# Rotary embedding on one core: a pair of slabs loaded in two halves of 64 partitions, the next pair in one load, and one table form for all slabs

## The chip, the core and the metric

The kernel runs on one NeuronCore of a Trainium2 chip. Its engines are TensorE (PE), VectorE (DVE), ScalarE (ACT), GpSimd (POOL) and SyncE (SP), each with an instruction stream of its own. 16 DMA engines move data between the memory outside the core (HBM) and the core's SBUF, which has 128 partitions. A DMA is cut into descriptors, each of which moves one contiguous run of bytes; the trace records each as a packet. DMAs are issued from an engine's stream: here the loads of x from SP, and the tables' loads and all stores from ACT. The metric is device time in microseconds (us), lower is better; a comparison is made on the median of several runs.

## The reference

A rotary position embedding: x is a float32 array of 16 batches x 512 positions x 1024 columns, seen as 16 heads of 64 columns. Each head's first 32 columns (x1) and last 32 (x2) are turned by a table of cosines and sines with one row for each position (512 x 32 each). x and the output are 33.55 MB each.

```python
x = x.reshape(batch, seq, num_heads, head_dim)
x1, x2 = x[..., :half_dim], x[..., half_dim:]
cos = cos[None, :, None, :]
sin = sin[None, :, None, :]
rotated = np.concatenate([
    x1 * cos - x2 * sin,
    x1 * sin + x2 * cos
], axis=-1)
```

## The kernel before

The 16 batches are worked on as 8 slabs of two batches, 4.19 MB each. On the 128 partitions a slab is a tile of 128 x 8192 float32 (`W`), 32 KB for each partition, that is 8 rows of x (`rpp`).

There are two layouts. Slabs 0, 1, 6 and 7 are contiguous in HBM: partition p holds rows 8p to 8p+7 of the slab (`dram`). Slabs 2 and 3, and 4 and 5, are halves of a pair: a pair is 8.39 MB, partition p holds 16 rows of it, 64 KB, and the two slabs are the first and the second 32 KB of each partition (`paired`). Two slab buffers (`slabs`, 32 KB a partition each) and two pair buffers (`pairs`, 64 KB each) take 192 KB of each partition.

Loads, all issued from SP: slabs 0 and 1 (line 68), then slabs 2 and 3 by one DMA whose descriptors are 64 KB (line 87), then 4 and 5 by one DMA each in 32 KB descriptors (line 90). These need no wait. Slabs 6 and 7 use the buffers of 0 and 1 again, so SP holds each of their loads until the store of slab 0, or 1, has landed (line 68 again, called from line 188).

Tables: cos and sin are loaded from ACT's queue into 64 partitions (line 83), 1 KB for each. POOL builds selection matrices (`pick`, `pick2`, lines 93 to 112) and casts the tables to bf16 (line 116). PE multiplies them so that each partition gets the rows that its positions need, with the sine's sign turned for the first half. There are two such tables: `tab` for the contiguous slabs (line 121, copied out by DVE at line 127), and `tab2` for both halves of a pair (line 133, copied out by ACT at line 172).

Passes: slab 0, 6 and 7 are worked on in two passes of 4 rows, the others in one pass of 8. A pass is a cast of the slab from float32 to bf16 in place on ACT (line 157), two multiplications by the tables and one addition on DVE (lines 175 and 176), and a cast back to float32 on ACT (line 179). ACT's order is fixed: the cast of the next pass comes before the cast back of this one. So when the next slab has not landed, the cast back of the present slab and its store wait behind it. After the last pass of a slab ACT issues its store (lines 182 to 186): 0, 1, 2, 3, 6 and 7 alone in 32 KB descriptors, 4 and 5 together in 64 KB descriptors.

Of the kernel before, what the change touches and what calls it, by code (L numbers as in the profile page):

```python
# [9 lines left out]
@with_exitstack  # L10
def kernel(
    ctx: ExitStack,
    tc: tile.TileContext,
    x: bass.AP,
    cos: bass.AP,
    sin: bass.AP,
    num_heads: int,
    out: bass.AP,
):
    nc = tc.nc  # L20
    P = nc.NUM_PARTITIONS

    batch, seq, dim = x.shape
    nh = num_heads
    hd = dim // nh
    half = hd // 2
    bf16 = mybir.dt.bfloat16
    f32 = mybir.dt.float32

    nb = 2  # L30
    nslabs = batch // nb
    rpp = nb * seq // P
    W = rpp * dim
    SP = seq // rpp
    TW = rpp * half

    out_flat = out.rearrange("b s h d -> b s (h d)")

    singles = ctx.enter_context(tc.tile_pool(name="singles", bufs=1))
    slabs = ctx.enter_context(tc.tile_pool(name="slabs", bufs=2))  # L40
    pairs = ctx.enter_context(tc.tile_pool(name="pairs", bufs=2))
    psum = ctx.enter_context(tc.tile_pool(
        name="psum", bufs=1, space=bass.MemoryType.PSUM))


    def dram(t, s, a=0, n=W):
        return bass.AP(tensor=t.tensor, offset=t.offset + s * nb * seq * dim + a,
                       ap=[[W, P], [1, n]])


    def view(t, offset, *dims):
        return dataclasses.replace(t, offset=t.offset + offset,
                                   ap=[t.ap[0], *[list(d) for d in dims]])

    slab = {}


    def paired(t, s, a=0, n=2 * W):
        return bass.AP(tensor=t.tensor, offset=t.offset + s * nb * seq * dim + a,
                       ap=[[2 * W, P], [1, n]])


    def load(s):
        slab[s] = slabs.tile([P, W], f32, tag="slab", name="slab")
        nc.sync.dma_start(out=slab[s], in_=dram(x, s))  # L68


    def place(s):
        t = pairs.tile([P, 2 * W], f32, tag="pair", name="pair")
        slab[s], slab[s + 1] = view(t, 0, (1, W)), view(t, W, (1, W))
        return t


    load(0)


    cos_sb = singles.tile([SP, TW], f32, tag="cos_sb")  # L80
    sin_sb = singles.tile([SP, TW], f32, tag="sin_sb")
    for t, src in ((cos_sb, cos), (sin_sb, sin)):
        nc.scalar.dma_start(out=t, in_=bass.AP(
            tensor=src.tensor, offset=src.offset, ap=[[TW, SP], [1, TW]]))

    load(1)
    nc.sync.dma_start(out=place(2), in_=paired(x, 2))
    pair = place(4)
    for h in range(2):
        nc.sync.dma_start(out=slab[4 + h], in_=paired(x, 4, h * W, W))  # L90


    pick = singles.tile([SP, 2 * P], bf16, tag="pick")
    nc.gpsimd.memset(pick, 0.0)  # L94
    for g in range(2):
        part = view(pick, g * P, (SP, P // SP), (1, SP))
        nc.gpsimd.affine_select(  # L97
            out=part, in_=part, compare_op=mybir.AluOpType.not_equal,
            fill=1.0 - 2.0 * g, base=0, pattern=[[0, P // SP], [-1, SP]],
            channel_multiplier=1)  # L100

    pick2 = singles.tile([SP, 4 * P], bf16, tag="pick2")
    nc.gpsimd.memset(pick2, 0.0)  # L105
    for h in range(2):
        for g in range(2):
            part = view(pick2, (2 * h + g) * P, (SP // 2, 2 * P // SP), (1, SP // 2))
            nc.gpsimd.affine_select(  # L109
                out=part, in_=part, compare_op=mybir.AluOpType.not_equal,  # L110
                fill=1.0 - 2.0 * g, base=-h, pattern=[[0, 2 * P // SP], [-2, SP // 2]],
                channel_multiplier=1)

    tab1 = singles.tile([SP, 2 * TW], bf16, tag="tab1")
    for i, t in enumerate((cos_sb, sin_sb)):
        nc.gpsimd.tensor_copy(out=view(tab1, i * TW, (1, TW)), in_=t)  # L116

    acc = psum.tile([P, 2 * rpp * hd], f32, tag="acc")
    for i in range(2):
        for h in range(2):  # L120
            nc.tensor.matmul(  # L121
                view(acc, i * rpp * hd + h * half, (hd, rpp), (1, half)),
                view(pick, i * h * P, (1, P)),
                view(tab1, i * TW, (half, rpp), (1, half)),
                start=True, stop=True)
    tab = singles.tile([P, 2 * rpp * hd], bf16, tag="tab")
    nc.vector.tensor_copy(out=tab, in_=acc)  # L127

    acc2 = psum.tile([P, 4 * rpp * hd], f32, tag="acc2")
    for i in range(2):  # L130
        for r in range(2):
            for h in range(2):
                nc.tensor.matmul(  # L133
                    view(acc2, (2 * i + r) * rpp * hd + h * half, (hd, rpp), (1, half)),
                    view(pick2, (2 * r + i * h) * P, (1, P)),
                    view(tab1, i * TW, (half, rpp), (1, half)),
                    start=True, stop=True)
    tab2 = singles.tile([P, 4 * rpp * hd], bf16, tag="tab2")

    passes = []
    for s in range(nslabs):
        n = rpp if 1 <= s < nslabs - 2 else rpp // 2
        passes += [(s, r, n) for r in range(0, rpp, n)]


    def halves(u):
        s, r, n = u  # L150
        t = view(slab[s], 0, (1, W)).bitcast(bf16)
        return [view(t, (2 * r + i * n) * dim, (1, n * dim)) for i in range(2)]


    def cast(u):
        s, r, n = u
        nc.scalar.copy(out=halves(u)[0], in_=view(slab[s], r * dim, (1, n * dim)))  # L157


    def factor(u, i):  # L160
        s, r, n = u
        t, a = (tab2, (2 * i + s % 2) * rpp * hd) if 2 <= s < 6 else (tab, i * rpp * hd)
        return view(t, a + r * hd, (hd, n), (0, nh), (1, hd))


    cast(passes[0])
    for i, u in enumerate(passes):
        s, r, n = u
        if i + 1 < len(passes):
            cast(passes[i + 1])  # L170
        if i == 0:
            tc.keep_in_program_order(nc.scalar.copy(out=tab2, in_=acc2))  # L172
        lo, up = halves(u)
        for k, t in enumerate((up, lo)):
            nc.vector.tensor_mul(out=t, in0=lo, in1=factor(u, k))  # L175
        nc.vector.tensor_add(  # L176
            out=up, in0=up, in1=view(lo, half, (hd, n * nh), (-half, 2), (1, half)))

        nc.scalar.copy(out=view(slab[s], r * dim, (1, n * dim)), in_=up)  # L179
        if r + n == rpp:  # L180
            if s == 5:
                nc.scalar.dma_start(out=paired(out_flat, 4), in_=pair)
            elif s in (2, 3):
                nc.scalar.dma_start(out=paired(out_flat, 2, (s - 2) * W, W), in_=slab[s])
            elif s != 4:
                nc.scalar.dma_start(out=dram(out_flat, s), in_=slab[s])
            if s < 2:
                load(s + 6)

# [34 lines left out]
```

## Time and profile before

| what | value |
|---|---|
| median of 3 runs | 166.65 us (164.38 to 167.47) |
| the profiled execution, whole | 161.82 us |
| its span from first to last instruction | 160.0 us |
| ACT busy | 115.1 us |
| DVE busy | 108.4 us |
| PE busy | 2.9 us |
| packets on the load queue | 1008, 33.55 MB |
| packets on ACT's queue (stores and tables) | 1168, 33.69 MB |

The profile is of one execution. Lines of the page name the source line (L157), the engine, the operation, what it writes and reads, its busy time, and the idle time of its engine before it with what ended it. Engine names with a q (SPq, ACTq) stand for the engine's instruction queue, which issues DMAs. "us to landing" is the time from a DMA's issue until its completion was signalled; it includes waiting behind other DMAs of its queue. Rows by stretch give, after the bounds and the length, the busy time of PE, PE's weight loads, DVE, ACT and POOL with their instruction counts, then the granted TensorE clock, the mean busy share of the 16 DMA engines and the GB/s that they moved. A packet is counted in the stretch in which it starts, so short stretches can show more than 1.0.

### The profile page before, as it was taken

The page shows a single profiled execution, that of the slowest core. Times are in us where ns is not written, and L with a number is a line of the kernel's source. Part 1 is how long each engine was busy: PE and PEld are TensorE (multiplying, and loading weights), DVE is VectorE, ACT ScalarE, POOL GpSimd, SP SyncE. Part 2 cuts the span into 40 slices and gives each one's busy share as a digit, 9 for nine tenths or more (in the row PEclk, how much of TensorE's full clock was granted, in tenths as well). Part 3 has the DMA queues.
Part 4 walks back from the last instruction along what each step waited for, and adds up shares of the span by engine and source line. Part 5 has one row for each costly group of instructions (what it writes and reads, how often), then busy time and mean ns, then how long its engine had stood idle before and what let it go on. Part 6 is the DMA issues. An engine that isn't in the chain of part 4 may idle for free.

```text
span 160.0 us, 179 instructions
## 1 busy us (share of the span) xinstructions
PE 2.9 (2%) x12; PEld 1.6 (1%) x12; DVE 108.4 (68%) x34; ACT 115.1 (72%) x24; POOL 3.3 (2%) x14
## 2 busy tenths in 40 slices
PE   0001410000000000000000000000000000000000
PEld 0000300000000000000000000000000000000000
DVE  0000299999971999899899989999279399910000
ACT  3005979994099999999999999399993999380000
POOL 6000000000000000000000000000000000000000
DMA  7999999699699999999999999999998998999994
GB/s 246 410 410 410 393 524 491 295 524 491 295 393 491 426 393 442 459 410 418 459 434 393 475 442 393 450 459 401 442 491 377 524 410 377 393 459 459 393 450 205
DMA packets 2176, 67.24 MB, mean 420 GB/s; under 512 B 256, under 2 KB 384, under 8 KB 384
## 3 DMA queue, kind: packets, MB, share of 16 engines
q1 hardware_dynamic: 1008, 33.55, 49.3%
q10 hardware_dynamic: 1168, 33.69, 48.8%
HBM read 33.69 MB, written 33.55 MB: 420 GB/s over the span
## 4 chain that ended last, share of the span: by engine, by line
DMA 67%; ACT 13%; issue 5%; DVE 4%; SPq 1%; ACTq 0%
DMA pair<-in_x_dram 27%; DMA slab<-in_x_dram 26%; DMA out_dram<-slab 15%; ACT slab L179 9%; DVE slab L175 3%; ACT slab L157 3%; ACT pair L157 2%; DVE slab L176 1%; SPq L68 1%; ACTq L179 0%; ACTq L157 0%
## 5 line engine op out<-in xcount | busy, mean ns | idle before, releaser
L175 DVE TENSOR_TENSOR slab<-slab,tab 128x4096 bf16<-128x4096 bf16 (+1 forms) x14 | 36.2, 2594 | 7.0 <-ACT slab L157 6.6
L157 ACT CAST slab<-slab 128x4096 bf16<-128x4096 f32 (+1 forms) x7 | 28.5, 4090 | 17.0 <-DMA slab<-in_x_dram 17.0
L175 DVE TENSOR_TENSOR pair<-pair,tab 128x8192 bf16<-128x8192 bf16 x8 | 35.4, 4424 | 6.2 <-ACT pair L157 6.0
L157 ACT CAST pair<-pair 128x8192 bf16<-128x8192 f32 x4 | 28.1, 7015 | 6.6 <-DMA pair<-in_x_dram 6.6
L179 ACT CAST slab<-slab 128x4096 f32<-128x4096 bf16 (+1 forms) x7 | 28.5, 4090 | 3.5 <-DVE slab L176 3.5
L179 ACT CAST pair<-pair 128x8192 f32<-128x8192 bf16 x4 | 28.1, 7016 | 0.3 <-DVE pair L176 0.3
L176 DVE TENSOR_TENSOR slab<-slab 128x4096 bf16<-128x4096 bf16 (+1 forms) x7 | 18.2, 2596 | 0.2
L176 DVE TENSOR_TENSOR pair<-pair 128x8192 bf16<-128x8192 bf16 x4 | 17.7, 4425 | 0.1
L127 DVE CAST tab<-acc 128x1024 bf16<-128x1024 f32 x1 | 1.2, 1224 | 18.8 <-PE acc L121 18.8
L157 ACT ACT_TABLE_LOAD x1 | 1.3, 1283 | 2.0 <-issue 2.0
L133 PE MATMUL acc<-tab,pick 64*128 64x256 bf16 x8 | 1.9, 414 | 0.0
L172 ACT CAST tab<-acc 128x2048 bf16<-128x2048 f32 x1 | 1.9, 1857 | 0.0
L121 PE MATMUL acc<-tab,pick 64*128 64x256 bf16 x4 | 1.2, 392 | 17.6 <-POOL tab L116 17.6
L133 PEld LDWEIGHTS <-pick 64*128 64x128 bf16 x8 | 1.1, 143 | 0.6
L109 POOL TENSOR_SCALAR_AFFINE_SELECT pick<-pick 64x128 bf16<-64x128 bf16 x4 | 1.1, 301 | 0.0
L121 PEld LDWEIGHTS <-pick 64*128 64x128 bf16 x4 | 0.5, 112 | 17.8 <-issue 15.9
L116 POOL CAST tab<-cos_sb 64x256 bf16<-64x256 f32 x1 | 0.4, 389 | 9.3 <-DMA cos_sb<-in_cos_dram 9.3
L97 POOL TENSOR_SCALAR_AFFINE_SELECT pick<-pick 64x128 bf16<-64x128 bf16 x2 | 0.5, 287 | 0.0
L105 POOL MEMSET pick<- 64x512 bf16 x1 | 0.5, 522 | 0.0
L116 POOL CAST tab<-sin_sb 64x256 bf16<-64x256 f32 x1 | 0.4, 394 | 4.9 <-DMA sin_sb<-in_sin_dram 4.9
L94 POOL MEMSET pick<- 64x256 bf16 x1 | 0.3, 304 | 0.3 <-POOLq L205 0.3
L205 POOL MEMSET const-bfloat16-1.0<- 128x1 bf16 x1 | 0.1, 111 | 0.0
(3 smaller groups left out, 0.3 us busy)
## 6 DMA issues: line engine op xcount, KB each, us to landing
slab<-in_x_dram SPq DMA_DIRECT2D x4, 4096.0 KB, 31.9
out_dram<-slab ACTq DMA_DIRECT2D x4, 4096.0 KB, 21.4
pair<-in_x_dram SPq DMA_DIRECT2D x2, 4096.0 KB, 71.0
out_dram<-pair ACTq DMA_DIRECT2D x2, 4096.0 KB, 31.8
cos_sb<-in_cos_dram ACTq DMA_DIRECT2D x1, 64.0 KB, 11.6
sin_sb<-in_sin_dram ACTq DMA_DIRECT2D x1, 64.0 KB, 16.4
pair<-in_x_dram SPq DMA_DIRECT2D x1, 42.7
out_dram<-pair ACTq DMA_DIRECT2D x1, 26.4
```

What stands on the lines that cost most here:

```text
L68: nc.sync.dma_start(out=slab[s], in_=dram(x, s))
L97: nc.gpsimd.affine_select(out=part, in_=part, compare_op=mybir.AluOpType.not_equal, fill=1.0 - 2.0 * g, base=0, pattern=[[0, P // SP], [-1 ...
L109: nc.gpsimd.affine_select(out=part, in_=part, compare_op=mybir.AluOpType.not_equal, fill=1.0 - 2.0 * g, base=-h, pattern=[[0, 2 * P // SP] ...
L116: nc.gpsimd.tensor_copy(out=view(tab1, i * TW, (1, TW)), in_=t)
L121: nc.tensor.matmul(view(acc, i * rpp * hd + h * half, (hd, rpp), (1, half)), view(pick, i * h * P, (1, P)), view(tab1, i * TW, (half, rpp) ...
L127: nc.vector.tensor_copy(out=tab, in_=acc)
L133: nc.tensor.matmul(view(acc2, (2 * i + r) * rpp * hd + h * half, (hd, rpp), (1, half)), view(pick2, (2 * r + i * h) * P, (1, P)), view(tab ...
L157: nc.scalar.copy(out=halves(u)[0], in_=view(slab[s], r * dim, (1, n * dim)))
L172: tc.keep_in_program_order(nc.scalar.copy(out=tab2, in_=acc2))
L175: nc.vector.tensor_mul(out=t, in0=lo, in1=factor(u, k))
L176: nc.vector.tensor_add(out=up, in0=up, in1=view(lo, half, (hd, n * nh), (-half, 2), (1, half)))
L179: nc.scalar.copy(out=view(slab[s], r * dim, (1, n * dim)), in_=up)
```

## The change

All eight slabs become halves of pairs. There are three pair buffers; slab s lies in half s % 2 of buffer s // 2 % 3, so slabs 6 and 7 use the two halves of the buffer of 0 and 1. In HBM each pair is laid out as 2-3 and 4-5 were. One pair of tables (`tabs[0]` for first halves, `tabs[1]` for second halves) serves all slabs; the table for contiguous slabs, with its selection matrices, matmuls and copy, is gone. `tabs[0]` is copied out by DVE and `tabs[1]`, half as wide as `tab2` was, by ACT.

The loads of slabs 0, 1, 6 and 7 are one DMA each, with 32 KB descriptors, now at a pitch of 64 KB in HBM. The load of slabs 2 and 3 becomes two DMAs, one for partitions 0 to 63 and one for partitions 64 to 127, each with 64 descriptors of 64 KB. The loads of slabs 4 and 5 become one DMA of 128 partitions with 64 KB descriptors. Stores are as before but for the layout: 4 and 5 together, the others alone. Passes, their order and the arithmetic are the same.

```diff
-    slabs = ctx.enter_context(tc.tile_pool(name="slabs", bufs=2))
-    pairs = ctx.enter_context(tc.tile_pool(name="pairs", bufs=2))
+    pairs = ctx.enter_context(tc.tile_pool(name="pairs", bufs=3))
...
+    places = [pairs.tile([P, 2 * W], f32, tag="pair", name="pair") for _ in range(3)]
...
+    def here(s, n=1):
+        return view(places[s // 2 % 3], s % 2 * W, (1, n * W))
...
+    def there(t, s, n=1):
+        return bass.AP(tensor=t.tensor, offset=t.offset + s // 2 * 2 * P * W + s % 2 * W,
+                       ap=[[2 * W, P], [1, n * W]])
...
+    def load(s, n=1):
+        nc.sync.dma_start(out=here(s, n), in_=there(x, s, n))
...
+    def store(s, n=1):
+        nc.scalar.dma_start(out=there(out_flat, s, n), in_=here(s, n))
...
     load(1)
-    nc.sync.dma_start(out=place(2), in_=paired(x, 2))
-    pair = place(4)
-    for h in range(2):
-        nc.sync.dma_start(out=slab[4 + h], in_=paired(x, 4, h * W, W))
+    for p in range(0, P, P // 2):
+        part = slice(p, p + P // 2)
+        nc.sync.dma_start(out=here(2, 2)[part], in_=there(x, 2, 2)[part])
+    load(4, 2)
...
-    pick = singles.tile([SP, 2 * P], bf16, tag="pick")
+    pick = singles.tile([TP, 4 * P], bf16, tag="pick")
...
+    accs, tabs = [], []
+    for h in range(2):
+        acc = psum.tile([P, 2 * rpp * hd], f32, tag=f"acc{h}", name="acc")
+        for i in range(2):
+            for f in range(2):
                 nc.tensor.matmul(
-                    view(acc2, (2 * i + r) * rpp * hd + h * half, (hd, rpp), (1, half)),
-                    view(pick2, (2 * r + i * h) * P, (1, P)),
+                    view(acc, i * rpp * hd + f * half, (hd, rpp), (1, half)),
+                    view(pick, (2 * h + i * f) * P, (1, P)),
                     view(tab1, i * TW, (half, rpp), (1, half)),
                     start=True, stop=True)
...
+    nc.vector.tensor_copy(out=tabs[0], in_=accs[0])
...
-            tc.keep_in_program_order(nc.scalar.copy(out=tab2, in_=acc2))
+            tc.keep_in_program_order(nc.scalar.copy(out=tabs[1], in_=accs[1]))
...
             if s == 5:
-                nc.scalar.dma_start(out=paired(out_flat, 4), in_=pair)
-            elif s in (2, 3):
-                nc.scalar.dma_start(out=paired(out_flat, 2, (s - 2) * W, W), in_=slab[s])
+                store(4, 2)
             elif s != 4:
-                nc.scalar.dma_start(out=dram(out_flat, s), in_=slab[s])
+                store(s)
```

More of the change, by code (lines that the diff above doesn't have):

```diff
@@ L33 @@
     W = rpp * dim
-    SP = seq // rpp
+    TP = seq // rpp
     TW = rpp * half
@@ L39 @@
     singles = ctx.enter_context(tc.tile_pool(name="singles", bufs=1))
-    slabs = ctx.enter_context(tc.tile_pool(name="slabs", bufs=2))
-    pairs = ctx.enter_context(tc.tile_pool(name="pairs", bufs=2))
+    pairs = ctx.enter_context(tc.tile_pool(name="pairs", bufs=3))
     psum = ctx.enter_context(tc.tile_pool(
         name="psum", bufs=1, space=bass.MemoryType.PSUM))
-    def dram(t, s, a=0, n=W):
-        return bass.AP(tensor=t.tensor, offset=t.offset + s * nb * seq * dim + a,
-                       ap=[[W, P], [1, n]])
     def view(t, offset, *dims):
@@ L53, in view @@
                                    ap=[t.ap[0], *[list(d) for d in dims]])
[L58 to L74, printed above, removed]
+    places = [pairs.tile([P, 2 * W], f32, tag="pair", name="pair") for _ in range(3)]
@@ L77 @@
+    def here(s, n=1):
[7 more added lines that the diff above has]
+        nc.scalar.dma_start(out=there(out_flat, s, n), in_=here(s, n))
     load(0)
-    cos_sb = singles.tile([SP, TW], f32, tag="cos_sb")
@@ L81 @@
-    sin_sb = singles.tile([SP, TW], f32, tag="sin_sb")
+    cos_sb = singles.tile([TP, TW], f32, tag="cos_sb")
+    sin_sb = singles.tile([TP, TW], f32, tag="sin_sb")
     for t, src in ((cos_sb, cos), (sin_sb, sin)):
         nc.scalar.dma_start(out=t, in_=bass.AP(
-            tensor=src.tensor, offset=src.offset, ap=[[TW, SP], [1, TW]]))
+            tensor=src.tensor, offset=src.offset, ap=[[TW, TP], [1, TW]]))
     load(1)
-    nc.sync.dma_start(out=place(2), in_=paired(x, 2))
-    pair = place(4)
@@ L89 @@
-    for h in range(2):
-        nc.sync.dma_start(out=slab[4 + h], in_=paired(x, 4, h * W, W))
-    pick = singles.tile([SP, 2 * P], bf16, tag="pick")
-    nc.gpsimd.memset(pick, 0.0)
[L95 to L104, printed above, removed]
@@ L105 @@
-    nc.gpsimd.memset(pick2, 0.0)
+    for p in range(0, P, P // 2):
[3 more added lines that the diff above has]
+    pick = singles.tile([TP, 4 * P], bf16, tag="pick")
+    nc.gpsimd.memset(pick, 0.0)
     for h in range(2):
         for g in range(2):
-            part = view(pick2, (2 * h + g) * P, (SP // 2, 2 * P // SP), (1, SP // 2))
+            part = view(pick, (2 * h + g) * P, (TP // 2, 2 * P // TP), (1, TP // 2))
@@ L109 @@
             nc.gpsimd.affine_select(
                 out=part, in_=part, compare_op=mybir.AluOpType.not_equal,
-                fill=1.0 - 2.0 * g, base=-h, pattern=[[0, 2 * P // SP], [-2, SP // 2]],
+                fill=1.0 - 2.0 * g, base=-h, pattern=[[0, 2 * P // TP], [-2, TP // 2]],
                 channel_multiplier=1)
-    tab1 = singles.tile([SP, 2 * TW], bf16, tag="tab1")
+    tab1 = singles.tile([TP, 2 * TW], bf16, tag="tab1")
     for i, t in enumerate((cos_sb, sin_sb)):
         nc.gpsimd.tensor_copy(out=view(tab1, i * TW, (1, TW)), in_=t)
-    acc = psum.tile([P, 2 * rpp * hd], f32, tag="acc")
@@ L119 @@
[L119 to L132, printed above, removed]
+    accs, tabs = [], []
@@ L137 @@
                     start=True, stop=True)
-    tab2 = singles.tile([P, 4 * rpp * hd], bf16, tag="tab2")
+        accs.append(acc)
+        tabs.append(singles.tile([P, 2 * rpp * hd], bf16, tag=f"tab{h}", name="tab"))
+    nc.vector.tensor_copy(out=tabs[0], in_=accs[0])
     passes = []
@@ L150, in halves @@
         s, r, n = u
-        t = view(slab[s], 0, (1, W)).bitcast(bf16)
+        t = here(s).bitcast(bf16)
         return [view(t, (2 * r + i * n) * dim, (1, n * dim)) for i in range(2)]
@@ L156, in cast @@
         s, r, n = u
[L157 to L163, printed above, removed]
+        nc.scalar.copy(out=halves(u)[0], in_=view(here(s), r * dim, (1, n * dim)))
     cast(passes[0])
@@ L171 @@
         if i == 0:
-            tc.keep_in_program_order(nc.scalar.copy(out=tab2, in_=acc2))
+            tc.keep_in_program_order(nc.scalar.copy(out=tabs[1], in_=accs[1]))
         lo, up = halves(u)
-        for k, t in enumerate((up, lo)):
-            nc.vector.tensor_mul(out=t, in0=lo, in1=factor(u, k))
+        for t, a in ((up, 0), (lo, rpp * hd)):
+            nc.vector.tensor_mul(
+                out=t, in0=lo,
+                in1=view(tabs[s % 2], a + r * hd, (hd, n), (0, nh), (1, hd)))
         nc.vector.tensor_add(
             out=up, in0=up, in1=view(lo, half, (hd, n * nh), (-half, 2), (1, half)))
-        nc.scalar.copy(out=view(slab[s], r * dim, (1, n * dim)), in_=up)
+        nc.scalar.copy(out=view(here(s), r * dim, (1, n * dim)), in_=up)
         if r + n == rpp:
             if s == 5:
-                nc.scalar.dma_start(out=paired(out_flat, 4), in_=pair)
-            elif s in (2, 3):
-                nc.scalar.dma_start(out=paired(out_flat, 2, (s - 2) * W, W), in_=slab[s])
+                store(4, 2)
             elif s != 4:
-                nc.scalar.dma_start(out=dram(out_flat, s), in_=slab[s])
+                store(s)
             if s < 2:
```

## The prediction

> **What bounds the kernel now.** I read the page first: its busy times, its forty slices with the DMA rows, and the chain that ended last.
>
> ```profile
> PE 2.9 (2%) x12; PEld 1.6 (1%) x12; DVE 108.4 (68%) x34; ACT 115.1 (72%) x24; POOL 3.3 (2%) x14
> DMA  7999999699699999999999999999998998999994
> HBM read 33.69 MB, written 33.55 MB: 420 GB/s over the span
> DMA 67%; ACT 13%; issue 5%; DVE 4%; SPq 1%; ACTq 0%
> ```
>
> No engine is near full, the DMA engines are in every slice (a packet counts where it starts, so a 6 stands beside overfull ones), and two thirds of the chain is DMA. The stretches say whether the transfers run at a fixed rate. In these rows the last two columns are the DMA share and GB/s.
>
> ```profile
> 24.00:40.00 16.00, 0.00 (x0) 0.00 (x0) 15.93 (x7) 13.83 (x3) 0.00 (x0) 1.00 1.04 451
> 44.00:118.00 74.00, 0.00 (x0) 0.00 (x0) 63.85 (x17) 70.67 (x12) 0.00 (x0) 1.00 1.00 432
> 121.00:138.00 17.00, 0.00 (x0) 0.00 (x0) 13.97 (x7) 14.22 (x4) 0.00 (x0) 1.00 1.00 432
> 141.00:157.00 16.00, 0.00 (x0) 0.00 (x0) 0.00 (x0) 3.38 (x1) 0.00 (x0) 1.00 1.00 430
> ```
>
> Loads alone (24 to 40, long packets cut by the window's edge), loads and stores mixed (44 to 118), 64 KB stores (121 to 138) and 32 KB stores (141 to 157): always share 1.0 and about 432 GB/s. That is 27.0 GB/s for each of 16 DMA engines, so a 32 KB descriptor takes 1.21 us and a 64 KB one 2.42 us of its engine, and a slab of 4.19 MB 9.7 us of all. The whole 67.24 MB need 67.24 / 0.432 = 155.6 us; the span is 160.0. What is left, 4.4 us, is the first issue, the ramp and the last landing. **The DMA engines set the end**, and compute matters only where it lets a queue run dry. The timeline gives that slack.
>
> ```profile
> 23.80 7.02 ACT L157 CAST slab<-slab 128x8192 bf16<-128x8192 f32 x1 [1.08 <-DMA slab<-in_x_dram]
> 37.86 0.35 ACTq L186 DMA_DIRECT2D out_dram<-slab  x1
> 44.40 7.02 ACT L157 CAST pair<-pair 128x8192 bf16<-128x8192 f32 x1 [6.57 <-DMA pair<-in_x_dram]
> 58.37 0.34 ACTq L186 DMA_DIRECT2D out_dram<-slab  x1
> 61.34 20.86 SPq L68 DMA_DIRECT2D slab<-in_x_dram  x2
> 72.08 7.01 ACT L157 CAST pair<-pair 128x8192 bf16<-128x8192 f32 x1
> 102.48 3.61 ACT L157 CAST slab<-slab 128x4096 bf16<-128x4096 f32 x1 [2.62 <-DMA slab<-in_x_dram]
> 113.45 0.34 ACTq L182 DMA_DIRECT2D out_dram<-pair  x1
> 123.09 3.60 ACT L157 CAST slab<-slab 128x4096 bf16<-128x4096 f32 x1 [2.66 <-DMA slab<-in_x_dram]
> 144.41 0.34 ACTq L186 DMA_DIRECT2D out_dram<-slab  x1
> ```
>
> ACT waits 6.57 us for the pair 2-3, and 2.62 and 2.66 us for slabs 6 and 7. The last store is issued at 144.41, while the store of slab 6 still has until about 149 to run (160.0 less 1.3 of landing, less 9.7): 4.6 us in hand.
>
> **The change, part by part.**
>
> *One table form.* Four of twelve matmuls go (4 x 0.41 us), a memset (0.30) and two selects (0.53) of POOL, and L172's copy falls from 2048 to 1024 columns, 1.86 to about 0.9 us. All are nothing for the end: POOL waits 9.3 us for the cos table anyway, the first table's matmuls and DVE copy (1.22) stay as they are, and ACT has 6.57 us of waiting right behind the copy. Without that cover ACT would gain 0.9 us.
>
> *Slabs 0, 1, 6, 7 in halves of a pair.* Three pairs of 64 KB fill the same 192 KB as two slabs and two pairs. Pieces of 32 KB at a pitch of 64 KB are what slabs 4 and 5 are loaded by and 2 and 3 stored by already, inside the row of 432 GB/s: no cost. Load 6 goes into the half that slab 0 leaves while slab 1 sits in the other. If dependences went by whole tiles, slab 1 would wait for it; but before, slab 3 is written at 79.00 while the store of slab 2, issued at 72.21 with 26 us to landing, reads the other half. No wait is added.
>
> *Slabs 4 and 5 in one load of 64 KB descriptors.* Eight packets of 2.42 us for each engine replace sixteen of 1.21: the same bytes and time. What moves is the sharing. Load and store queues take turns by packet, seen in the even split between 43 and 61 us (load queue 54.0% of the engines, store queue 47.2%), when load 4 and store 0 are out together. With 64 against 32 KB the load gets two thirds. A turn of both lasts 3.63 us, so without the other edit slabs 4 and 5 would land together after 42.3 + 8 x 3.63 = 71.3, about 72.4 with the landing, where ACT needs slab 4 at 72.08. Store 0 ends near 69 instead of 60, so load 6, which SP holds for it, is issued at about 70 instead of 61.34 (load 7, behind it on SP, at about 90 instead of 81.9). But slab 5 no longer lies ahead of them: load 6 takes 8 turns of 2.42 from 71 and lands near 92 (needed at 99.9), load 7 near 111 (needed at 120.4). Both ACT waits go. At the end nothing comes of it, since the DMA engines are full with or without: 0 us.
>
> *Slabs 2 and 3 in two loads of 64 partitions.* The same 128 descriptors of 64 KB, one more issue (0.42 us on SP, with nothing due behind it). The tables' loads are the only ones of 64 partitions, and they ran on all 16 engines (the page's 256 packets under 512 B are 16 completion packets for each of 16 transfers, the tables' two among them). So each of 16 engines gets 4 + 4 packets. What one packet costs when only half of the partitions are addressed is the unknown that decides. **Lower end**: the 64 KB packet of today's pair load, 2.42 us, no cost. **Upper end**: every row at 432 GB/s addresses all 128 partitions, 3.4 GB/s each; if the partitions' side sets the rate, half of them take 216 GB/s, 4.84 us a packet. The only rows of 64 partitions are these tables:
>
> ```profile
> cos_sb<-in_cos_dram ACTq DMA_DIRECT2D x1, 64.0 KB, 11.6
> sin_sb<-in_sin_dram ACTq DMA_DIRECT2D x1, 64.0 KB, 16.4
> ```
>
> 64 KB in 11.6 us beside a slab of 4096 KB that landed 13.1 us after its issue. They take turns with it and have pieces of 1 KB, so they set no price; but they are nearest in partition count, and they do not show half the partitions running at full rate. The rate is the same in both directions and for both sizes, so it is a ceiling of something that all large transfers share: the engines or the full set of partitions. I take the upper end, without certainty.
>
> The sum by the upper end: load 2-3a runs from 22.9 (slab 1's cast at 23.80, less 0.9 of landing) to 42.3, where today the whole pair ends (9.7 us lost), load 2-3b to 61.7 (again 9.7). Store 0, issued at 37.86, takes a turn between b's packets; while one engine stores, its 1.21 us fall into the time that the loads wait for each other. Four turns hide 4.85 us. **Loss: 19.4 - 4.85 = 14.5 us**; 19.4 if nothing is hidden. What is late next: slab 2's cast moves from 44.40 to 63.8, and behind it on ACT slab 1's last copy and store 1 (58.37 to 77.8) and everything after. Slabs 4 to 7 are in time, 7's wait of 2.66 goes, 6's is taken by DVE (its add for slab 5 ends 19.4 later too). The last store is issued at 144.41 + 19.4 - 2.66 = 161.2, and the DMA engines reach it at 149 + 14.5 = 163.5; store 4-5 at 132.9 against 119.5 + 14.5 = 134.0. Both in time, with 1 to 2 us in hand, so the sum stands at 14.5. The profiled execution is 161.82: 176.3. The median of the runs is 166.65, 4.8 above it with the same work, and I carry that offset: **181 us**.
>
> [...]
>
> **Rivals.**
>
> *The engines are the ceiling.* A 64-partition packet costs 2.42 us as today. For it: 27.0 GB/s an engine holds in every stretch, and all 16 engines stay in use. Then all parts sum to nothing: 166.5, not slower.
>
> *Earlier landings bring a gain.* The runs stand 2.6 to 5.7 us above the profiled execution. If in them a queue ran dry because slabs 6 and 7 came late, the landings pulled forward by 10 us would bring it back: 162 to 163, over 2% faster. It decides only if the half loads cost under about 1 us and if store 7 was late by more than its 4.6 us in hand. Against it: the profile shows no such gap, and gains nothing from these waits.
>
> *Half price.* Only one of the two half loads is slowed, or the engines drift apart so that two seldom meet: 5 to 10 us, 172 to 176.
>
> **How the numbers follow.** Upper end 0.55 (176 to 186: from 9.7 lost to all 19.4); half price 0.09; engines as ceiling 0.20; gain 0.16. The range from 164 to 187 leaves out the gain and a few in a hundred at the top. The likeliest case's own range is 176 to 187. About 2% (3.3 us) is what the runs, which lie between 164.38 and 167.47, can tell from no change: slower 0.64, same 0.20, faster 0.16.
>
> **What would show it.** If right: ACT's wait for the pair 2-3 grows from 6.6 to about 26 us, slab 2's cast starts near 64, the slices from 23 to 42 us fall to about half the GB/s at full DMA share, and the waits for slab 7 vanish. If that wait stays at 6 to 7 us and the slices at 430, the price of half the partitions is nothing and the forecast falls. If the cast starts at 64 and yet the end moves by far more than 14.5, a queue ran dry behind ACT. The part on slabs 4 and 5 shows in load 6: issued 8 to 15 us later than 61.34, with no ACT wait for it.

## The result and the profile after

The changed kernel takes 183.88 us (median of 6 runs, 183.55 to 184.14). Its ratio to the kernel before is 1.134, with a 95% interval of 1.130 to 1.137: slower by 13.4%. The profiled execution took 183.55 us with a span of 181.8, where the one before had 161.82 and 160.0: 21.8 us more span. The median before, over all runs taken beside it, is 164.69; some of those runs were slower than the rest and the ratio leaves them out, so it is larger than the quotient of the two medians.

First the page of the changed kernel: the DMA engines' slices, the two queues with the share of 16 engines' time that their packets took, the bytes, and the chain that ended last.

```profile
DMA  6989965999949989998999999999994999988995
q1 hardware_dynamic: 880, 33.55, 53.7%
q10 hardware_dynamic: 1168, 33.69, 43.4%
HBM read 33.69 MB, written 33.55 MB: 370 GB/s over the span
DVE 35%; ACT 30%; issue 13%; another core or an unknown queue 8%; DMA 6%; PE 0%; POOLq 0%; ACTq 0%; POOL 0%; DVEq 0%
```

The same queue lines of the kernel before:

```profile
q1 hardware_dynamic: 1008, 33.55, 49.3%
q10 hardware_dynamic: 1168, 33.69, 48.8%
```

The bytes are the same. Before, packets filled 98.1% of 160.0, or 157.0 us of each DMA engine; after, 97.1% of 181.8, or 176.5 us. So **19.5 of the 21.8 us are transfers that take longer**. The time in which the engines moved nothing, a mean over the 16, rose from 3.0 to 5.3 us: **2.3 us are engines without work**. The chain no longer names the DMA engines first. That is no evidence that compute became the limit: the chain is followed back from the last instruction of ACT, and the 19.5 us lie in transfers that it passes by. The kernel with the whole pair in one load (the first experiment below) is as fast as the kernel before, and its chain names ACT first as well:

```profile
ACT 36%; DMA 27%; DVE 13%; issue 13%; another core or an unknown queue 1%; SPq 0%; ACTq 0%
```

The stretches of the changed kernel show where (last columns: DMA share, GB/s).

```profile
22.40:42.40 20.00, 0.00 (x0) 0.00 (x0) 19.90 (x8) 14.03 (x3) 0.00 (x0) 1.00 1.02 213
42.40:65.00 22.60, 0.00 (x0) 0.00 (x0) 3.99 (x1) 7.02 (x1) 0.00 (x0) 1.00 0.98 255
65.00:137.00 72.00, 0.00 (x0) 0.00 (x0) 56.19 (x14) 55.45 (x9) 0.00 (x0) 1.00 1.00 431
137.40:141.60 4.20, 0.00 (x0) 0.00 (x0) 3.02 (x2) 4.20 (x2) 0.00 (x0) 1.00 0.42 179
```

In the first 20 us, with the first half load alone, all 16 engines are busy (1.02) and move 213 GB/s instead of 432; a single packet of 64 KB takes 5.12 us, against 2.42. In the second, the other half load beside store 0, it is 255. Once the pair has landed the rate is back at 431, mixed with 64 KB loads. At 137 to 142 the share falls to 0.42, as the store queue has run dry and the loads are done. The timeline tells why:

```profile
46.42 7.02 ACT L151 CAST pair<-pair 128x8192 f32<-128x8192 bf16 x1 [8.64 <-DVE pair L148]
67.75 13.94 ACT L133 CAST pair<-pair 128x8192 bf16<-128x8192 f32 x2 [14.31 <-DMA pair<-in_x_dram]
74.80 13.22 DVE L145 TENSOR_TENSOR pair<-pair,tab 128x8192 bf16<-128x8192 bf16 x3 [28.42 <-ACT pair L133]
87.94 4.42 DVE L148 TENSOR_TENSOR pair<-pair 128x8192 bf16<-128x8192 bf16 x1
92.45 7.02 ACT L151 CAST pair<-pair 128x8192 f32<-128x8192 bf16 x1 [10.76 <-DVE pair L148]
140.74 0.34 ACTq L69 DMA_DIRECT2D out_dram<-pair  x1
```

Two things differ from the kernel before, although the source gives the same order: ACT's order, called fixed above, is not. ACT casts slab 1 back (46.42) ahead of slab 2's cast and then casts slabs 2 and 3 in a row. DVE does three multiplications in a row: two of slab 2, then one of slab 3, and only then slab 2's addition (87.94). So slab 2's cast back waits 10.76 us, and the store of 4 and 5, issued at 113.45 before, comes at 140.74. The order in the built program has changed, without a line of the source asking for it. Why it changed is not shown.

### The profile page after: what moved, and what is told of

Read it like the earlier page. It is cut to its first block, busy times and chain, and to the rows that moved or that the text cites. A ratio compares the mean times of both kernels' runs of the same rounds, so it can differ in the third digit from the quotient of the medians.

```text
span 181.8 us, 167 instructions
## 1 busy us (share of the span) xinstructions
PE 2.0 (1%) x8; PEld 1.0 (1%) x8; DVE 108.1 (59%) x34; ACT 114.3 (63%) x24; POOL 2.6 (1%) x11
## 4 chain that ended last, share of the span: by engine, by line
DVE 35%; ACT 30%; issue 13%; another core or an unknown queue 8%; DMA 6%; PE 0%; POOLq 0%; ACTq 0%; POOL 0%; DVEq 0%
DVE pair L145 25%; ACT pair L151 18%; ACT pair L133 12%; DVE pair L148 10%; DMA cos_sb<-in_cos_dram 6%; DVE tab L114 1%; PE acc L107 0%; POOLq L189 0%; POOL tab L100 0%; ACTq L69 0%; ACTq L151 0%; DVEq L145 0%; ACTq L133 0%
## 5 line engine op out<-in xcount | busy, mean ns | idle before, releaser
L145 DVE TENSOR_TENSOR pair<-pair,tab 128x4096 bf16<-128x4096 bf16 (+1 forms) x22 | 71.5, 3259 | 38.7 <-ACT pair L133 38.2
L133 ACT CAST pair<-pair 128x4096 bf16<-128x4096 f32 (+1 forms) x11 | 56.5, 5152 | 26.8 <-DMA pair<-in_x_dram 26.8
L151 ACT CAST pair<-pair 128x4096 f32<-128x4096 bf16 (+1 forms) x11 | 56.6, 5154 | 26.0 <-DVE pair L148 26.0
L148 DVE TENSOR_TENSOR pair<-pair 128x4096 bf16<-128x4096 bf16 (+1 forms) x11 | 35.9, 3260 | 0.3
L107 PE MATMUL acc<-tab,pick 64*128 64x256 bf16 x8 | 2.0, 405 | 17.1 <-POOL tab L100 17.1
L107 PEld LDWEIGHTS <-pick 64*128 64x128 bf16 x8 | 1.0, 130 | 17.6 <-issue 15.6
L93 POOL TENSOR_SCALAR_AFFINE_SELECT pick<-pick 64x128 bf16<-64x128 bf16 x4 | 1.1, 302 | 0.1
L142 ACT CAST tab<-acc 128x1024 bf16<-128x1024 f32 x1 | 1.0, 1002 | 0.0
```

The source lines that it names most:

```text
L93: nc.gpsimd.affine_select(out=part, in_=part, compare_op=mybir.AluOpType.not_equal, fill=1.0 - 2.0 * g, base=-h, pattern=[[0, 2 * P // TP] ...
L107: nc.tensor.matmul(view(acc, i * rpp * hd + f * half, (hd, rpp), (1, half)), view(pick, (2 * h + i * f) * P, (1, P)), view(tab1, i * TW, ( ...
L133: nc.scalar.copy(out=halves(u)[0], in_=view(here(s), r * dim, (1, n * dim)))
L142: tc.keep_in_program_order(nc.scalar.copy(out=tabs[1], in_=accs[1]))
L145: nc.vector.tensor_mul(out=t, in0=lo, in1=view(tabs[s % 2], a + r * hd, (hd, n), (0, nh), (1, hd)))
L148: nc.vector.tensor_add(out=up, in0=up, in1=view(lo, half, (hd, n * nh), (-half, 2), (1, half)))
```

## The experiments

**One part undone: the whole pair in one load.**

```diff
-    for p in range(0, P, P // 2):
-        part = slice(p, p + P // 2)
-        nc.sync.dma_start(out=here(2, 2)[part], in_=there(x, 2, 2)[part])
+    load(2, 2)
```

> The changed kernel with one part undone: slabs 2 and 3 by one load of 128 partitions with 64 KB descriptors; the single layout, the one table form and the single load of slabs 4 and 5 stay. If the half loads are the whole cost: span 159.5 to 160.5 us (160.0 before, 181.8 changed), ACT's wait for slab 2 back to 6 to 7 us, no ACT wait over 1 us for slabs 6 and 7, load 6 issued near 70 us. Rival, the layout or the 64 KB load of 4 and 5 carries a part of it (load 6 held back by a slower store 0): span 163 us or more, with a stretch in which the DMA engines are not full.

Measured: span 160.2, ratio to before 0.998 (0.995 to 1.001).

```profile
44.47 7.02 ACT L131 CAST pair<-pair 128x8192 bf16<-128x8192 f32 x1 [6.95 <-DMA pair<-in_x_dram]
69.88 20.84 SPq L65 DMA_DIRECT2D pair<-in_x_dram  x2
73.49 7.02 ACT L131 CAST pair<-pair 128x8192 bf16<-128x8192 f32 x1 [1.24 <-DMA pair<-in_x_dram]
114.86 0.34 ACTq L69 DMA_DIRECT2D out_dram<-pair  x1
```

ACT waits 6.95 us for slab 2. Load 6 is issued at 69.88 and load 7 at 90.4, and ACT waits for neither; slab 4 costs it 1.24 us. So the layout, the one table form and the 64 KB load of 4 and 5 are worth nothing together, and all the loss hangs on the two half loads. The earlier landing of slabs 6 and 7 brings no time, as the DMA engines are full anyway (share 1.01 from 44.5 to 71.5 us). The built program has the order of the kernel before.

**One part alone: only the half loads.**

```diff
-    nc.sync.dma_start(out=place(2), in_=paired(x, 2))
+    pair = place(2)
+    for p in range(0, P, P // 2):
+        part = slice(p, p + P // 2)
+        nc.sync.dma_start(out=pair[part], in_=paired(x, 2)[part])
```

> The kernel before with one part of the change alone: slabs 2 and 3 by two loads of 64 partitions. If the half loads are the whole cost: 18 to 22 us more than before (span 178 to 182), with 64 KB packets of the half loads at about 205 GB/s over all engines between 23 and 43 us. Rival, the cost needs the long turns of the 64 KB load of 4 and 5 beside it: at most 15 us more.

Measured, in one execution: span 179.9, 19.9 us more, with 213 GB/s between 22.4 and 42.4 us. The cost needs nothing else of the change. The order of the built program moved here too, DVE again taking three multiplications in a row:

```profile
74.88 13.22 DVE L178 TENSOR_TENSOR pair<-pair,tab 128x8192 bf16<-128x8192 bf16 x3 [28.20 <-ACT pair L160]
135.95 0.34 ACTq L185 DMA_DIRECT2D out_dram<-pair  x1
```

But the store of 4 and 5 is issued at 135.95, in time, and the DMA engines do not run empty (every slice of the page from 68 to 157 us reads 9).

**The disputed cost by itself: which partitions.** A kernel that only loads and stores, each transfer after the one before, 64 KB for each partition.

> Transfers by themselves, one after another, 64 KB for each partition; all computation is left out, and only parts of the output are written. Loads in order: partitions 0-127, 0-63, 32-95, 64-127, 96-127, 0-127, 0-31, 16-47; then stores of 0-127, 0-63, 32-95, 0-31 with a load of 128 x 1 KB before each. [...] Rival one, the rate goes with the number of partitions: 432, 216, 216, 216, 108, 432, 108, 108. Rival two, the half loads were slow only for what ran beside them: all loads of 64 partitions near 400 here. [...]

The stretches of this run, which is one execution, one line for each transfer in the order just given (8 loads, 4 stores); the last number is GB/s, over a stretch from the first packet's start to the last one's end.

```profile
1.60:22.40 20.80, 0.00 (x0) 1.00 0.96 403
24.00:44.90 20.90, 0.00 (x0) 1.00 0.97 201
46.70:57.60 10.90, 0.00 (x0) 1.00 0.93 385
59.10:80.10 21.00, 0.00 (x0) 1.00 0.96 200
81.80:92.60 10.80, 0.00 (x0) 1.00 0.92 194
94.00:114.60 20.60, 0.00 (x0) 1.00 0.97 407
115.80:126.70 10.90, 0.00 (x0) 1.00 0.92 192
128.10:138.60 10.50, 0.00 (x0) 1.00 0.95 200
142.30:162.00 19.70, 0.00 (x0) 1.00 0.99 426
165.70:186.40 20.70, 0.00 (x0) 1.00 0.99 203
190.00:199.90 9.90, 0.00 (x0) 1.00 0.98 424
203.20:213.60 10.40, 0.00 (x0) 1.00 0.98 202
```

Lines 2 and 3 are both 64 partitions: 0-63 at 201 GB/s, 32-95 at 385 (by length and share of the row 2.5 us a packet, as with 128 partitions in line 1). Lines 5, 7 and 8 are 32 partitions, and with 194, 192 and 200 GB/s about as fast as 64 of one side: the number of partitions doesn't set the rate, which rules out rival one. Nothing ran beside, which rules out rival two. Nor is it the HBM side: 0-63 and 32-95 each read one contiguous piece of 4.19 MB. The stores show the same pattern (lines 9 to 12: 426, 203, 424 and 202 GB/s). Every slow set lies on one side of partition 64 (192 to 203 GB/s) and every fast one on both (385 to 426). What makes it so is not shown. Where the expectations below say ports, that is the author's name for a cause in the set of partitions; no run shows a port.

**The order alone.** The changed kernel with DVE's order pinned at one place, that is, held to the order of the source by `keep_in_program_order`.

```diff
-            nc.vector.tensor_mul(
+            ins = nc.vector.tensor_mul(
...
+            if s == 3 and a == 0:
+                tc.keep_in_program_order(ins)
```

> The changed kernel with one order pinned: DVE's add of slab 2 before its first multiplication of slab 3, as in the kernel before. If the dry stretch of the DMA engines near 140 us comes from this swapped order: slab 2's cast back starts 4.4 us earlier (88.0 instead of 92.45), the store of 4 and 5 is issued near 136.4 instead of 140.7, the dry stretch goes, span 179.3 to 179.9 (181.8 changed). Rival, the late pair alone runs the queue dry, whatever the order: 181 to 182.

Measured: span 180.1, 181.87 us, ratio 1.122 (1.120 to 1.124). Slab 2's cast back starts at 88.67, as expected. The store of 4 and 5 is issued at 138.5, not 136.4: slab 4's cast, no longer held by ACT, now waits 1.44 us for its load. From 136 to 140 us the DMA share is 1.12, where the changed kernel had 0.42 from 137.4 to 141.6. So 1.7 of the 21.8 us of span came from this one swap.

**Another cut of the pair.** With the same pin, and

```diff
-    for p in range(0, P, P // 2):
-        part = slice(p, p + P // 2)
+    for p, q in ((32, 96), (0, 32), (96, 128)):
+        part = slice(p, q)
```

> The changed kernel with the pinned order of the run before it (the add of slab 2 before the first multiplication of slab 3; span 180.1 with halves 0-63 and 64-127), and the pair 2-3 cut at other partitions: 32-95, then 0-31, then 96-127. Ports: the middle half runs at 2.42 us a packet, the other four packets of each engine at 5.12, so 4 x 2.7 = 10.8 us lost instead of 19.5: span 169.5 to 172. Rival, any cut of the pair costs, whatever the partitions: 180 or more, as three loads instead of two.

Measured, in one execution: span 170.1, 9.9 us above the whole pair and 10.0 below the halves. Three loads cost half of what two cost. What counts is which partitions a load holds.

**What a store hides.** The whole pair 2-3, and

```diff
-    load(4, 2)
+    for p in range(0, P, P // 2):
+        part = slice(p, p + P // 2)
+        nc.sync.dma_start(out=here(4, 2)[part], in_=there(x, 4, 2)[part])
```

> The kernel with the whole pair 2-3 (span 160.2), and now the pair 4-5 loaded in halves 0-63 and 64-127, so that every one of the 8 half-load packets of an engine takes turns with a store packet. The prediction counted 1.21 us of each such turn as hidden: 4.84 against 3.63 us a turn, 9.7 us lost, span 169 to 171. [...] What ACT does later in this run may add a dry stretch of the DMA engines, to be read off by itself.

Measured, in one execution: span 179.4, 19.2 us lost, where the prediction's way of counting gave 9.7. From 44.5 to 91 us the engines are busy (share 1.01) and move 264 GB/s, where with the whole pair 4-5 they move 439 from 44.5 to 71.5. The reason shows in the DMA queues of the changed kernel, in two stretches of 1.1 us one after the other. From 47.1 to 48.2, the packets that started (count, MB, share):

```profile
q10 hardware_dynamic: 16, 0.52, 125.3%
```

and from 48.3 to 49.4:

```profile
q1 hardware_dynamic: 16, 1.05, 415.7%
```

Sixteen packets in each, as many as there are DMA engines, and by the shares each takes longer than the stretch (1.38 and 4.57 us): first all engines take a packet of the store, then all take one of the load. A turn takes about 4.6 us for the load and 1.4 for the store, 6.0 together, where 4.84 was counted; one after the other without mixing, 5.12 and 1.21, they are 6.3. Put end to end by their times, the packets up to 65 us form 16 rows, as many as there are engines: 13 of them begin each load within 0.7 us of one another and take 4.4 to 4.7 us for it. The three that run ahead of these take less from turn to turn, 3.8 to 4.0 us at the last, so for these three a store does hide something. In the run with halves of 4 and 5 eight such turns, each 2.4 us above the 3.63 of a full load and a store, make 19 us.

**Two queues, steps, and one queue.** Transfers by themselves again, in one execution.

> Transfers by themselves; all computation is left out, and only the first quarter of the output is written. First partitions 0-63 from SP's queue and 64-127 from ACT's queue at once: if the engines stay in step, all at the low half and then all at the high half, about 205 GB/s and 41 us together; if the two queues let the halves run beside each other, 432 GB/s and 20 us. [...] Then 32-95, 0-31 and 96-127 one behind the other on one queue: 9.7 + 10.2 + 10.2 = 30 us. Last 0-127 as a check, and its store.

```profile
2.00:41.80 39.80, 0.00 (x0) 1.00 0.98 211
43.70:54.70 11.00, 0.00 (x0) 1.00 0.93 381
56.20:66.00 9.80, 0.00 (x0) 1.00 1.05 428
66.00:86.90 20.90, 0.00 (x0) 1.00 0.95 201
```

Line 1: two half loads from two queues at once move 211 GB/s together, little more than one alone. Line 2 is one load of the 64 even partitions, for which 205 or 432 GB/s had been put: 381, by length and share of the row 2.6 us a packet, near the 385 of 32-95 in the run above. The trace doesn't tell which engine takes which partitions, so why it is fast stays open. Lines 3 and 4: 32-95 at 428, then 0-31 and 96-127 at 201.

**The same two half loads on other partitions.** If the set of partitions is all, the change needs only other halves:

```diff
-    for p in range(0, P, P // 2):
-        part = slice(p, p + P // 2)
+    for p in range(2):
+        part = slice(p, P, 2)
```

> The changed kernel with one thing different: the two loads of 64 partitions for slabs 2 and 3 take the even and the odd partitions instead of 0-63 and 64-127. Still two DMAs of 64 descriptors of 64 KB, and the same order of instructions on ACT and DVE as in the changed kernel. [...] Rival, two DMAs of 64 partitions cost as such: 180 to 182. In between, if the later cast back of slab 2 alone runs the DMA engines dry: 161 to 164.

Measured: span 168.2, ratio 1.043 (1.033 to 1.053): above the 161 to 164 of the case in between and the 160 to 161 expected of loads at full rate alone, and below the rival's 180. The loads are cured: 430 GB/s between 22.6 and 42.2, and the queue lines say 93.3% of 168.2, 156.9 us of packets as before. But the order of the built program is still that of the changed kernel, and it costs 8 us here:

```profile
78.84 7.02 ACT L151 CAST pair<-pair 128x8192 f32<-128x8192 bf16 x1 [10.76 <-DVE pair L148]
127.15 0.34 ACTq L69 DMA_DIRECT2D out_dram<-pair  x1
```

and the stretch ahead of that store:

```profile
119.70:127.90 8.20, 0.00 (x0) 0.00 (x0) 7.09 (x4) 7.80 (x2) 0.00 (x0) 1.00 0.00 0
```

Slab 2's cast back comes at 78.84, where the kernel with the whole pair has it at 65.24; the store of 4 and 5 comes 12.3 us later than there (114.86), and the DMA engines move nothing for 8.2 us.

**The order pinned, with either kind of halves.** Both engines get the order of the kernel before: slab 2's addition ahead of slab 3's first multiplication as above, and

```diff
-        nc.scalar.copy(out=view(here(s), r * dim, (1, n * dim)), in_=up)
+        ins = nc.scalar.copy(out=view(here(s), r * dim, (1, n * dim)), in_=up)
+        if s == 1:
+            tc.keep_in_program_order(ins)
```

With even and odd partitions:

> The kernel with even and odd partitions (span 168.2, with the DMA engines empty from 119.7 to 127.9 us), and ACT and DVE pinned to the order of the kernel with the whole pair: slab 1's cast back behind slab 2's cast, slab 2's add before slab 3's first multiplication. If the 8 us come from the order alone: the store of 4 and 5 issued near 115 instead of 127.2, no empty stretch, span 160.0 to 160.6. Rival, loads by even and odd partitions themselves delay something: 163 or more.

With partitions 0-63 and 64-127:

> The changed kernel (halves 0-63 and 64-127, span 181.8) with the same two pins, so that both engines keep the order of the kernel before. This is the case that the prediction worked out. Ports alone: 160.2 + 19.5 = 179.7 if no dry stretch is left; slab 2's cast near 68, store 1 near 82, the store of 4 and 5 near 115 + 23 = 138 where the DMA engines come to it at about 139: span 179.3 to 180.5. Rival, the order hardly matters here: 181.5 to 182.

Measured: 159.9 (ratio 0.998, 0.995 to 1.001) and 179.9 (1.120, 1.116 to 1.125). Two loads of 64 partitions cost nothing when they take the even and the odd ones, each from both sides of 64, and the order is kept. With the halves of the change and the order kept, the loss is 20.0 us, nearly all of it in packets (98.3% of 179.9 is 176.8 us). The timeline of this last one is the case that the prediction worked out:

```profile
67.99 7.02 ACT L133 CAST pair<-pair 128x8192 bf16<-128x8192 f32 x1 [30.42 <-DMA pair<-in_x_dram]
81.96 0.34 ACTq L69 DMA_DIRECT2D out_dram<-pair  x1
137.08 0.34 ACTq L69 DMA_DIRECT2D out_dram<-pair  x1
```

| half loads | order as built | order of the kernel before |
|---|---|---|
| even and odd partitions | 168.2 | 159.9 |
| partitions 0-63 and 64-127 | 181.8 | 179.9 |

The two costs don't add up. The order alone costs 8.3 us, but only 1.9 beside slow loads, since the DMA engines then run out of other work some 20 us later (near 140 us instead of 120) and wait only 1.8 us for the store of 4 and 5.

## Why the prediction was right, and where it was off

**The bound.** Right. The DMA engines set the end, and where the queue lines were read (before, after, half loads alone, even and odd partitions in either order, halves with the order kept), the span is the time of the packets plus 3.0 to 3.4 us, and the dry stretch where there is one (2.3 us after, 8.2 with even and odd partitions in the order as built).

**One table, layout, 64 KB load of 4 and 5: nothing.** Right, by the kernel with the whole pair (160.2). The figures along the way hold as well: load 6 was put at about 70 and load 7 at about 90 (69.88 and 90.4), and slab 4 was put at 72.4 with its landing, 0.3 us behind the cast's time (the wait was 1.24).

**The upper end for the half loads.** Right in kind. It was taken over a lower end of no cost with no row to decide; the partition sets decide it. The reason given with it, a rate per partition, is wrong: 32 partitions are about as fast as 64 of one side (192 to 200 GB/s against 200 and 201), and 64 across both sides run nearly at the rate of 128 (385 against 403 and 407, 430 in the kernel). 4.84 us a packet was 6% low; it is 5.12 while the half load has the engines to itself, and 4.87 where two half loads took turns (0.98 of 39.80 us for eight packets).

**"Four turns hide 4.85 us."** This is the step that failed. The loss of transfers is 19.5 us, not 14.5. It was assumed that a store's 1.21 us fall into time in which loads wait for each other; no run shows such a wait. Nearly all the engines are in step, a turn takes 6.0 us instead of 4.84, and next to nothing is hidden, here and in the run with halves for 4 and 5. The price of 19.4 without hiding, which the prediction kept for its range, was the better middle.

**What is late next.** Put at 63.8 for slab 2's cast, measured 67.75, by the same two errors. The order of ACT and DVE was taken over from the kernel before. The built program's order was another: its store of 4 and 5 came 7.8 us after the 132.9 put for it, 4.2 of them by the late pair (137.08 with the order kept) and the rest by the order, and 2.3 us without work followed. A queue run dry was named as what would take the end beyond the loads' own price; it wasn't priced.

**The signs that were named.** The stretch from 22.4 to 42.4 us has about half the GB/s at full DMA share, and ACT no longer waits for slab 7, as foretold. ACT's wait for the pair is 14.31 us instead of about 26, since slab 1's cast back now runs ahead of it; with the order kept it is 30.42. Load 6 was to come 8 to 15 us later than 61.34: it is 8.5 with the whole pair, but 20.9 in the changed kernel (82.21), where store 0 takes turns with the half loads. One reading in the part on the layout is wrong, without harm to it: the store of slab 2 took 29.0 us to landing, not 26, which is the time of the store of slabs 4 and 5.

**The number.** 181 against 183.88 is nearer than the working deserves, by luck: two errors of opposite sign. The loss was put 7.3 us too low (14.5, measured 21.8 of span), and 4.8 us too much was carried over: the offset of the median before from its profiled execution isn't there after (183.88 against 183.55), nor in the kernel with the whole pair (162.0).

**The rivals.** The engines as ceiling: refuted by the half loads' 201 GB/s, with a packet at 5.12 us. A gain from earlier landings: refuted by the kernel with the whole pair, which has the landings and no gain. Half price: both half loads were slow (213 GB/s alone, 255 beside the store); 9.9 us was met only by a cut that wasn't the change's.

## What to carry to other kernels

When the DMA engines are full, ask of each transfer not how many partitions or descriptors it has but which partitions: here a cut at 64 halved the rate of both parts (201 and 200 GB/s against 403), and a cut into even and odd ones (430 in the kernel), or around the middle for the part 32 to 95 (385 and 428), cost that part next to nothing. Don't count a transfer of the other direction as cover for a load slowed in this way: here nearly all the engines took turns in step, 6.0 us each, and it hid next to nothing. And after any change to a load's form, look at the order of the built program on each engine before a wait is explained: here it moved by itself and was worth 8.3 us once the loads were cured.

## What was not expected of the hardware

All 16 engines were shown busy at a share of 0.97 while they moved 201 GB/s: a full DMA share is no proof of a full rate. A turn between the two queues was one descriptor, be it of 64 or of 32 KB. Between 46 and 68 us of the kernel with the whole pair, loads and stores started 96 packets each, and the loads had two thirds of the engines' time:

```profile
q1 hardware_dynamic: 96, 6.29, 65.9%
q10 hardware_dynamic: 96, 3.15, 33.1%
```

Open: why partitions of one side of 64 are slow, why a packet of a half load takes 5.12 us and not the 4.84 of the estimate, why 4.87 when two queues take turns, which engine takes which partitions in a load of 64, and why the built order moves with the form of a load. None of these was tried further.
